# Splitting the weight transfers of one expert by rows in a hybrid attention and mixture-of-experts block

## Chip, cores and metric

The kernel runs on one core of a Trainium2 chip. The metric is the device time of one execution in microseconds (us), here the median of three runs. The profile is of one execution, with its own time.

## What is computed

One decoder block on 256 tokens of width 1024 in float32. Two attention branches (dilated, and a sliding window with sinks) share one input projection, are gated and added to `x`; then comes a mixture of 32 experts in 4 groups, of which each token uses two, and a last norm. The part that matters here:

```python
def hier_moe(h, w_group, b_group, w_router, b_router, w_e_gate, w_e_up, w_e_down):
    ...
    out = jnp.zeros_like(hf)
    for e in range(N_EXPERTS):
        a = jax.nn.silu(hf @ w_e_gate[e]) * (hf @ w_e_up[e])
        out = out + gates[:, e:e + 1].astype(hf.dtype) * (a @ w_e_down[e])
    return out.reshape(b, t, d)
```

`w_e_gate` and `w_e_up` are 1024 x 512 for each expert, `w_e_down` is 512 x 1024: 6 MB an expert, 192 MB in all.

## The kernel before

The first part of the program (projection, attention, output projection, routing) takes a little less than half of the span. The second part goes over the 32 experts (NE = 32) one after the other. For each, up to 32 of its tokens are gathered, multiplied by the gate and up weights (`gateup`, tile `gu`), activated, turned (`finish`, tile `atp`), multiplied by the down weights (tile `dn`), scaled, and added into the four accumulators `quad`. Every matmul is recorded at L132, a helper. For the last two experts some matmuls on no new data are put between the others (`busy`, tile `idle`). Behind the last expert stand the norm and four stores.

The weights lie in HBM so that each expert is three pieces of 2 MB, each of 128 rows (one for each partition) of 16 KB in one run: two pieces of `w_e_gu` (gate and up together, half of the depth each) and one of `w_e_down`. In SBUF a piece goes to a tile `ew` of 128 partitions x 4096 float32. The places for these tiles form a ring of large buffers, which fills up as the first part lets go of them. `prefetch(n)` takes the next n pieces of `chunk_items`, each into the next place of the ring, and calls `fill`, which issues the transfers on SyncE's queue (SP). One transfer carries a whole piece; only for the last expert (e = NE - 1 = 31) is a piece cut, by columns: each `w_e_gu` piece into two of 1 MB, the `w_e_down` piece into one of 1 MB and two of 512 KB. The loop over the experts calls `prefetch(2)` after the gate and up products of an expert and `prefetch(1)` after its down product. After expert 30, the gain of the last norm is fetched into a tile `gf` (L1107). The framework puts the waits in: a transfer waits for its place to be free and for a semaphore of its own, and the products wait for all transfers into the tile that they read. The semaphores that transfers raise are used in turn.

Transfers of another shape stand at the start of the program: among them 128 rows of 512 B into `cs` and 8 rows of 512 B into `grow`, both on ScalarE's queue (ACTq, q10 in the profile), and 8 rows into `frow` on SyncE's (q1).

Of the kernel before, what the change touches and what calls it, by code (L numbers as in the profile page):

```python
# [17 lines left out]
P = 128  # L18
# [5 lines left out]
NE = 32  # L24
# [60 lines left out]
def tile_hybrid_block(  # L85
# [12 lines left out]
    V, A, PE, SP = nc.vector, nc.scalar, nc.tensor, nc.sync  # L98
# [558 lines left out]
    chunks = {}  # L657
    nchunk = [0]

    def fill(t, e, what, i):  # L660
        if what == 0:
            parts = 2 if e == NE - 1 else 1
            for j in range(parts):
                n = 2 // parts
                SP.dma_start(
                    t[:, 2048 * n * j:2048 * n * (j + 1)],
                    w_e_gu[e, i, :, n * j:n * (j + 1)].rearrange("p k u r c -> p (k u r c)"))
        else:
            for c0, c1 in (((0, 2), (2, 3), (3, 4)) if e == NE - 1 else ((0, 4),)):
                SP.dma_start(t[:, 1024 * c0:1024 * c1], w_e_down[e, :, c0:c1, :].rearrange("p c o -> p (c o)"))  # L670

    def next_place(name):
        nchunk[0] += 1
# [13 lines left out]
    def prefetch(n):  # L687
        for _ in range(n):
            m = nchunk[0]
            if m >= len(chunk_items):  # L690
                return
            e, what, i = chunk_items[m]
            t = next_place(f"ew{m}")
            fill(t, e, what, i)
            for h in range(2):
                chunks[(e, what, 2 * i + h)] = t[:, 2048 * h:2048 * h + 2048]
# [471 lines left out]
```

## Time and profile before

| what | value |
|---|---|
| median of 3 runs | 747.11 us (745.70 to 747.63) |
| profiled execution, own time | 745.13 us |
| its span, first to last instruction | 743.3 us |
| TensorE matmul busy | 625.0 us, 84% |
| VectorE, ScalarE busy | 296.0 us, 224.3 us |
| moved by DMA | 249.86 MB, mean 336 GB/s |

The profile's times count from the first instruction. The DMA share of a stretch is the mean busy share of the core's 16 DMA engines; it can come out a little over 1. The time to landing of a transfer counts from its issue to the last of its completions. The profile doesn't say on which of the 16 engines a packet ran.

### The profile page before, as it was taken

How to read it: one execution, taken by the hardware profiler on the slowest of the kernel's cores; microseconds unless marked ns; L12 is line 12 of the kernel's file. 1: busy time of each engine (PE TensorE's matmuls, PEld its weight loads, DVE VectorE, ACT ScalarE, POOL GpSimd, SP SyncE). 2: the span in 40 equal slices, each digit the busy share in tenths (PEclk: the TensorE clock that was granted, in tenths of full speed). 3: DMA queues.
4: the chain of work that ended last, by engine and by line, in shares of the span. 5: the costliest groups of instructions: out<-in, count | busy, mean ns of one | idle time of the engine just before them, and what ended most of it. 6: DMA issues, size and time to landing. Idle time of an engine off the chain costs nothing.

```text
span 743.3 us, 14685 instructions
## 1 busy us (share of the span) xinstructions
PE 625.0 (84%) x6416; PEld 459.2 (62%) x6416; DVE 296.0 (40%) x753; ACT 224.3 (30%) x448; POOL 2.1 (0%) x10
## 2 busy tenths in 40 slices
PE   9999999999999999999988777677676867777772
PEld 8999988888998998655545334344333534433331
DVE  6554767985788566532223112111211111111103
ACT  6444566775788444210101001000000000000004
POOL 0000000000000000000000000000000000000000
PEclk9999999999999999999999789989879887978797
DMA  8746346336537978999999999999999999999993
GB/s 325 282 176 227 142 142 225 116 115 237 217 114 304 381 276 309 405 395 429 427 425 428 426 424 428 425 427 425 428 429 422 428 427 427 427 426 427 428 410 113
DMA packets 25940, 249.86 MB, mean 336 GB/s; under 512 B 5120, under 2 KB 6544, under 8 KB 8336
## 3 DMA queue, kind: packets, MB, share of 16 engines
q1 hardware_dynamic: 25712, 248.81, 82.4%
q8 instruction: 52, 0.85, 0.5%
q14 instruction: 16, 0.13, 0.0%
q10 hardware_dynamic: 160, 0.07, 0.0%
HBM read 247.82 MB, written 1.05 MB: 335 GB/s over the span
## 4 chain that ended last, share of the span: by engine, by line
DMA 50%; PE 24%; DVE 5%; ACT 5%; issue 1%; SPq 0%; DVEq 0%
DMA ew<-in_w_e_gu_dram 31%; DMA ew<-in_w_e_down_dram 19%; PE acc L132 12%; PE gu L132 4%; PE quad L132 2%; DVE set_split L258 2%; ACT set_probs L514 1%; PE dn L132 1%; PE ga L132 1%; DVE set_probs L525 1%; PE dpv L132 1%; PE dtp L594 1%; ACT set_split L257 1%; DVE set_qs L410 1%; DVE set_probs L512 1%
## 5 line engine op out<-in xcount | busy, mean ns | idle before, releaser
L132 PE MATMUL gu<-ew,xes 128*32 128x256 f32 x2048 | 151.0, 427 | 43.1 <-DMA ew<-in_w_e_gu_dram 42.9
L132 PE MATMUL acc<-set_hT,set_split 128*128 128x256 f32 x1200 | 151.3, 281 | 0.8 <-DVE set_qa L410 0.8
L132 PEld LDWEIGHTS acc<-set_hT,set_split 128*128 128x128 f32 x1200 | 142.1, 188 | 2.7 <-DVE set_qa L410 1.0
L132 PEld LDWEIGHTS gu<-ew,xes 128*32 128x32 f32 x2048 | 67.5, 120 | 104.8 <-DMA ew<-in_w_e_gu_dram 56.4
L258 DVE TENSOR_TENSOR set_split<-set_raw,set_split 128x1024 fp32r<-128x1024 f32 (+1 forms) x84 | 100.2, 1198 | 33.8 <-ACT set_split L257 31.3
L257 ACT CAST set_split<-set_raw 128x1024 fp32r<-128x1024 f32 (+1 forms) x84 | 86.3, 1029 | 42.0 <-PE acc L132 41.1
L946 DVE TENSOR_TENSOR set_raw<-set_raw,gu 128x128 f32<-128x128 f32 x32 | 9.2, 286 | 193.0 <-ACT set_raw L943 192.9
L132 PE MATMUL dn<-ew,set_raw 128*32 128x256 f32 x1024 | 75.1, 435 | 9.8 <-DMA ew<-in_w_e_down_dram 9.4
L943 ACT ACTIVATE set_raw<-gu 128x128 f32<-128x128 f32 x32 | 8.9, 277 | 218.4 <-PE gu L132 218.4
L132 PEld LDWEIGHTS dn<-ew,set_raw 128*32 128x32 f32 x1024 | 34.9, 122 | 35.3 <-issue 10.8
L972 ACT ACTIVATE y_hi<-dn,gsl 128x256 fp32r<-128x256 f32 x32 | 15.2, 473 | 97.2 <-PE dn L132 97.2
L132 PE MATMUL ga<-set_raw 128*128 128x128 f32 x256 | 37.0, 304 | 5.2 <-DVE set_raw L959 4.2
L132 PEld LDWEIGHTS ga<-set_raw 128*128 128x128 f32 x256 | 33.7, 212 | 9.0 <-DVE set_raw L959 6.9
L974 DVE SCALAR_TENSOR_TENSOR y_lo<-dn,gsl,y_hi 128x256 fp32r<-128x256 f32 x32 | 15.4, 481 | 59.6 <-ACT y_hi L972 59.6
L881 ACT ACTIVATE xes<-ga,fcol 128x128 f32<-128x128 f32 x32 | 11.6, 367 | 76.0 <-DVE xes L883 76.0
L132 PE MATMUL acc<-set_split,set_hT 128*128 128x512 f32 x144 | 34.1, 393 | 0.4 <-DVE set_ks L420 0.2
L913 DVE TENSOR_SCALAR set_raw<-cs,pos 128x128 f32<-128x128 f32 x64 | 17.8, 281 | 37.9 <-PE ct L132 37.9
L132 PE MATMUL quad<-y_hi,cts 32*128 32x256 f32 x256 | 23.3, 350 | 9.1 <-ACT y_hi L972 9.1
L132 PEld LDWEIGHTS acc<-set_split,set_hT 128*128 128x128 f32 x144 | 26.7, 188 | 6.7 <-DVE set_split L258 0.6
L132 PEld LDWEIGHTS quad<-y_hi,cts 32*128 32x128 f32 x256 | 13.6, 200 | 22.1 <-ACT y_hi L972 20.6
L132 PE MATMUL quad<-y_lo,cts 32*128 32x256 f32 x256 | 21.5, 344 | 6.9 <-DVE y_lo L974 3.4
L138 PE MATMUL atp<-cs,set_raw 128*128 128x128 f32 x32 | 11.1, 346 | 19.0 <-DVE set_raw L946 18.2
(201 smaller groups left out, 632.8 us busy)
## 6 DMA issues: line engine op xcount, KB each, us to landing
ew<-in_w_e_gu_dram SPq DMA_DIRECT2D x62, 2048.0 KB, 39.1
ew<-in_w_e_down_dram SPq DMA_DIRECT2D x31, 2048.0 KB, 39.3
set_raw<-in_w_in_dram SPq DMA_DIRECT2D x29, 1024.0 KB, 5.3
set_raw<-in_w_br_swa_dram SPq DMA_DIRECT2D x4, 1024.0 KB, 4.9
set_raw<-in_w_out_dram SPq DMA_DIRECT2D x4, 1024.0 KB, 6.1
ew<-in_w_e_gu_dram SPq DMA_DIRECT2D x4, 1024.0 KB, 33.1
set_raw<-in_w_br_dil_dram SPq DMA_DIRECT2D x2, 1024.0 KB, 5.1
set_x<-in_x_dram SPq DMA_DIRECT2D x2, 512.0 KB, 4.4
```

The lines of the kernel that those rows point to most:

```text
L132: i = PE.matmul(o, lhsT, rhs, start=start, stop=stop, skip_group_check=True)
L138: i = PE.transpose(o, src, ident)
L257: order(A.copy(w[:, 0, :, :ncol], r))
L258: order(V.tensor_tensor(out=w[:, 1, :, :ncol], in0=r, in1=w[:, 0, :, :ncol].bitcast(F32), op=ALU.subtract))
L410: V.scalar_tensor_tensor(out=lo, in0=sv, scalar=cs[own, j:j + 1], in1=hi.bitcast(F32), op0=ALU.mult, op1=ALU.subtract)
L512: V.tensor_tensor_reduce(out=v, in0=s, in1=dist, scale=float(scale), scalar=init, op0=ALU.add, op1=ALU.min, accum_out=nm[:, i:i + 1])
L881: A.activation(dst, src, AF.Copy, scale=col)
L913: eq = V.tensor_scalar(dd[:, t, :].rearrange("p (g s) -> p g s", g=REP), cs[:, C_CNT:C_CNT + CAP].unsqueeze(1).to_broadcast([P, REP, CAP]) ...
L943: A.activation(ac, gu[:, 0:P], AF.Silu)
L946: V.tensor_tensor(out=ac, in0=ac, in1=gu[:, P:2 * P], op=ALU.mult)
L972: A.activation(y_hi, dn[:, 0:256], AF.Copy, scale=gsl)
L974: V.scalar_tensor_tensor(out=y_lo, in0=dn[:, 0:256], scalar=gsl, in1=y_hi.bitcast(F32), op0=ALU.mult, op1=ALU.subtract)
```

## The change

For the last expert but one (e = NE - 2 = 30), each of its three pieces goes out as three transfers in place of one: rows 0 to 111, rows 112 to 119, and rows 120 to 127. The bytes and the tiles are the same. All other transfers stay as they are.

```diff
+    def whole(t, src):
+        SP.dma_start(t, src)
+
+    def by_rows(t, src):
+
+        for a, b in ((0, 112), (112, 120), (120, P)):
+            SP.dma_start(t[a:b], src[a:b])
+
     def fill(t, e, what, i):
+        put = by_rows if e == NE - 2 else whole
         if what == 0:
             parts = 2 if e == NE - 1 else 1
             for j in range(parts):
                 n = 2 // parts
-                SP.dma_start(
+                put(
                     t[:, 2048 * n * j:2048 * n * (j + 1)],
                     w_e_gu[e, i, :, n * j:n * (j + 1)].rearrange("p k u r c -> p (k u r c)"))
         else:
             for c0, c1 in (((0, 2), (2, 3), (3, 4)) if e == NE - 1 else ((0, 4),)):
-                SP.dma_start(t[:, 1024 * c0:1024 * c1], w_e_down[e, :, c0:c1, :].rearrange("p c o -> p (c o)"))
+                put(t[:, 1024 * c0:1024 * c1], w_e_down[e, :, c0:c1, :].rearrange("p c o -> p (c o)"))
```

## Rows read from the trace of the kernel before

**Rows 1.** The page's 40 slices: busy tenths of TensorE, DMA share, GB/s

```profile
PE   9999999999999999999988777677676867777772
...
DMA  8746346336537978999999999999999999999993
GB/s 325 282 176 227 142 142 225 116 115 237 217 114 304 381 276 309 405 395 429 427 425 428 426 424 428 425 427 425 428 429 422 428 427 427 427 426 427 428 410 113
```

**Rows 2.** Chain of waits, 560 to 730 us: start us, length us, what

```profile
585.41 39.31 DMA ew<-in_w_e_down_dram
...
624.78 40.07 DMA ew<-in_w_e_gu_dram
...
664.90 3.47 PE gu L132 x32
...
670.19 39.12 DMA ew<-in_w_e_gu_dram
709.30 0.02 issue
709.32 19.84 DMA ew<-in_w_e_down_dram
729.16 0.04 issue
729.20 0.68 PE dn L132 x8
```

**Rows 3.** Waits of SyncE's queue, 560 to 716 us: total us, times, longest

```profile
SPq L665 <- DMA ew<-in_w_e_gu_dram: 50.7, 11, 5.6
SPq L670 <- DMA ew<-in_w_e_gu_dram: 45.1, 10, 4.5
SPq L665 <- DMA ew<-in_w_e_down_dram: 41.0, 9, 4.9
SPq L1107 <- DMA ew<-in_w_e_down_dram: 4.6, 1, 4.6
SPq L670 <- DMA ew<-in_w_e_down_dram: 4.6, 1, 4.6
SPq L665 <- PE ct L132: 0.5, 2, 0.3
SPq L670 <- PE ct L132: 0.3, 1, 0.3
SPq L670 <- PE dn L132: 0.2, 1, 0.2
```

**Rows 4.** Timeline of SyncE's queue, issues between 664 and 715 us

```profile
664.92 0.33 SPq L665 DMA_DIRECT2D ew<-in_w_e_gu_dram  x1
...
675.09 0.33 SPq L670 DMA_DIRECT2D ew<-in_w_e_down_dram  x1
679.99 0.33 SPq L665 DMA_DIRECT2D ew<-in_w_e_gu_dram  x1
...
704.43 0.33 SPq L670 DMA_DIRECT2D ew<-in_w_e_down_dram  x1
709.32 0.33 SPq L670 DMA_DIRECT2D ew<-in_w_e_down_dram  x1
714.27 0.33 SPq L1107 DMA_DIRECT2D gf<-in_g_final_dram  x1
```

**Rows 5.** Stretches: busy us of each engine, TensorE clock, DMA share, GB/s

```profile
620.00:719.00 99.00, 73.36 (x861) 40.57 (x853) 14.24 (x49) 6.72 (x18) 0.00 (x0) 0.83 1.01 426
...
723.00:724.00 1.00, 0.33 (x3) 0.12 (x2) 0.00 (x0) 0.00 (x0) 0.00 (x0) 1.00 0.94 385
724.00:725.00 1.00, 0.81 (x16) 0.42 (x16) 0.00 (x0) 0.00 (x0) 0.00 (x0) 1.00 0.83 340
725.00:726.00 1.00, 0.72 (x11) 0.32 (x4) 0.29 (x1) 0.65 (x2) 0.00 (x0) 1.00 0.59 229
726.00:727.00 1.00, 0.80 (x8) 0.56 (x12) 0.29 (x1) 0.99 (x2) 0.00 (x0) 1.00 0.50 188
727.00:728.00 1.00, 0.88 (x20) 0.34 (x16) 0.00 (x0) 0.12 (x1) 0.00 (x0) 1.00 0.51 205
728.00:728.40 0.40, 0.40 (x8) 0.10 (x8) 0.00 (x0) 0.00 (x0) 0.00 (x0) 1.00 0.49 195
728.40:728.80 0.40, 0.18 (x4) 0.00 (x0) 0.00 (x0) 0.00 (x0) 0.00 (x0) 1.00 0.49 195
728.80:729.20 0.40, 0.00 (x0) 0.00 (x1) 0.00 (x0) 0.00 (x0) 0.00 (x0) 1.00 0.35 143
729.20:730.00 0.80, 0.64 (x8) 0.16 (x8) 0.00 (x0) 0.09 (x1) 0.00 (x0) 1.00 0.23 92
```

**Rows 6.** DMA queues, 340 to 729 us: packets, MB, share of 16 engines

```profile
q8 instruction: 28, 0.46, 0.5%
```

**Rows 7.** DMA view, 0 to 20 us: a queue, and ScalarE's two issues

```profile
q10 hardware_dynamic: 160, 0.07, 1.8%
...
cs<-c_small_dram ACTq DMA_DIRECT2D x1, 64.0 KB, 3.5
...
grow<-in_g_mix_dram ACTq DMA_DIRECT2D x1, 4.0 KB
```

**Rows 8.** The page's DMA issues: count, KB each, median us to landing

```profile
ew<-in_w_e_gu_dram SPq DMA_DIRECT2D x62, 2048.0 KB, 39.1
ew<-in_w_e_down_dram SPq DMA_DIRECT2D x31, 2048.0 KB, 39.3
set_raw<-in_w_in_dram SPq DMA_DIRECT2D x29, 1024.0 KB, 5.3
```

## Prediction

> **What bounds the kernel now.** I read the page's slices first [rows 1]. From a third of the span on, the DMA row stands at 9 in every slice and the GB/s row between about 405 and 429, while TensorE's own row falls to 7 and 6: the second half is a stream of weights, and the engines wait for it. The chain of waits agrees [rows 2]: from 585 us it is transfers of some 39 us laid end to end, with a few microseconds of TensorE between two of them, and the last one, the final part of the last expert's down weights, lands at 729.16 us. What comes behind it (the last down product, the output product, the norm, the store) takes the rest of the 743.3 us, 14.1 us, and the change touches none of it. So the question is only when that last part lands.
>
> Next the queue that issues the transfers. SyncE waits almost always for a landing, and for TensorE only 1.0 us in all over 156 us [rows 3]. The issue times say which landing: the three pieces of the last expert but one are issued at 664.92, 670.19 and 675.09, the transfers eight issues behind them at 704.43, 709.32 and 714.27 [rows 2, 4], and the second of these follows the landing at 709.31 by 0.02 us [rows 2]. A transfer lands some 39 us after its issue [rows 8] and a piece takes 4.9 us, which is eight pieces. Eight transfers are in flight, whatever their size, and each landing lets one more go.
>
> Last the tail, cut fine [rows 5]. Up to 719 us the DMA share is 1.01 at 426 GB/s. From 723 it falls, and from 726 to 728.8 it stays at 0.49 to 0.51 with 188 to 205 GB/s. Half of the engines have nothing left, and the other half doesn't speed up: 205 over 0.51 is 402 GB/s for all sixteen, under the 426 of before (the rows are smaller there). So an engine has its own pace, 426/16/1.01 = 26.4 GB/s, and a row of 16 KB takes it 0.62 us. How far is the late half behind? Missing share from 723 to 728.4: 0.06 + 0.17 + 0.41 + 0.50 + 0.49 + 0.4 x 0.51 = 1.83 us of all engines, 3.7 us of half of them, so the early half ends at 724.7 on average. The late half's share after 728.4 is 0.4 x 0.49 + 0.4 x 0.35 + 0.8 x 0.23 = 0.52, 1.0 us of half of them, so it ends at 729.4. The lag is 4.7 us. A cause that fits: in the 389 us before, 28 instruction packets took 0.5% of sixteen engines' time [rows 6], which is 31 us, 3.9 us for each of eight engines and 1.9 for each of sixteen. The last transfer lands with the late half.
>
> **The change, part by part.** Expert 30 has three pieces, 128 rows of 16 KB each. Now a piece is one transfer, 8 rows for each of sixteen engines. After it is 112 rows, then 8, then 8.
>
> *112 rows.* Sixteen divides 112: 7 rows an engine, 0.62 us less on each engine and piece, 1.85 us over three.
>
> *The 8-row transfers.* The trace has an 8-row transfer: early on, ScalarE's queue moved 128 rows of 512 B and 8 more, in 160 packets [rows 7]. 136 of these are rows; the other 24 are completions, 16 for the large transfer and 8 for the small one. So 8 rows go to eight engines, one each. [...] Taking the same eight both times, a piece gives eight engines 9 rows and eight engines 7, and three pieces move 3 rows, 1.85 us, from one half to the other.
>
> *Which half.* No row names engines. If the loaded half is the early one, the late half ends 1.85 us sooner and the early half 1.85 us later, with 4.7 - 3.7 = 1.0 us of lag left: the last landing moves by -1.85. If it is the late one, by +1.85. I take the early one. The order in which the trace keeps packets that start together leans to it, but no view prints that, so it is a judgment: 5 to 1.
>
> *Six more issues on SyncE.* 0.33 us each [rows 4], 2 us in all, against 146 us of waits for landings in the 156 us [rows 3]: nothing.
>
> *Three landings to wait for.* TensorE's first product on a piece of expert 30 now waits for three transfers; the next products and expert 30's tail are queued behind it. From 620 to 719 us TensorE is busy 73 of 99 us [rows 5], so a shift of 2 us there is absorbed as long as the last expert's transfers aren't late themselves: nothing.
>
> *The eight places in flight.* The nine transfers fill more than the eight places, so what follows is issued later. The third part of expert 30's down piece must wait for the landing of the 112 rows of its first piece (704.43 before, some 0.6 sooner now), and the last expert's first transfer goes right behind it, at about 704.2 instead of 679.99 [rows 4]. When are they needed? Expert 30's down piece landed just ahead of 714.27; the late half gets there at about 712.4, the early half at 714.3 - 4.7 + 1.85 = 711.4. So the lead shrinks from 34 us to 7. A transfer of 1 MB into an idle queue needs 5.3 us to land [rows 8], of which 2.5 are its own data at 426 GB/s, so some 2.9 us of lead are enough. Nothing is lost; without that cover it would be 2 to 5 us once.
>
> *An 8-row transfer's own pace.* Its rows go to eight neighbouring partitions, from eight engines at a time. No large transfer of that shape stands in the trace. From below: 0.62 us, the pace that an engine holds whether eight or sixteen of them run [rows 5]. From above: the eight rows get no further than two at a time, four turns of 0.62, 2.46 us. I take the lower end, because rows 5 are nearest to it: there eight engines run and each keeps its pace.
>
> The sum against the profiled execution: last landing 729.16 - 1.85 = 727.3, span 741.5, its own time 745.13 - 1.85 = 743.3. That execution lies 1.98 us under the median of 747.11; from the median, the forecast is **745.3 us**, 0.25% faster. What a measurement here can tell from no change is about 0.3%, 2.2 us, so this would mostly read as no change.
>
> **Rivals.**
>
> *The 8-row transfers block (slower).* At the upper end each of the six costs 1.85 us more on the loaded half, 11.1 us. That half starts 4.7 us early and takes 1.85 us of added rows: -4.7 + 1.85 + 11.1 = +8.2 us, about 755. If the two small transfers of a piece overlap fully, 16 rows in four turns, the extra is 1.23 us a piece, 3.7 in all, and the end moves by +0.9; if the 112 rows, whose shares no longer fall as those of 128 do, hurt each other as well by half a row per engine and piece, another 1 us on top of the 8.2. It decides from an extra of 4.7 - 1.85 = 2.85 us, 0.48 us a small transfer. For it: the constant pace of rows 5 was seen only where each engine has a share of a transfer of 128 rows. Against it: nothing in the trace slows down when engines run out of step. [...]
>
> *The other half is loaded.* +1.85 us, 749.0. For it: no row names engines. Against it: only the judgment above.
>
> *Rows follow partitions.* If the engine goes by the partition that is written and not by the count, the sixteen rows of the two small transfers fall to the engines that had them before, and every engine still has 8 rows: 747.1. Against it: the eight completions in rows 7, which fit one row an engine.
>
> *The queue runs dry.* If the lead of 7 us is not enough, 2 to 5 us once: about 750. Against it: the 5.3 us of rows 8.
>
> **How the numbers follow.** Forecast (early half loaded, own pace) 0.42; blocking 0.40, spread over 748 to 757; other half 0.07; rows by partition 0.06; dry queue 0.05. The likeliest, 745.3, has its own range of 744.3 to 746.3, from the scatter of the three runs. About 3 in 10 of it would read faster than 0.3%: 0.13. No change: the rest of it 0.29, rows by partition 0.06, most of the other half 0.05, and a little of the blocking case where its transfers overlap, 0.02: 0.42. Slower: 0.45. The range runs from 744.3 to 757: it leaves out the lower edge of the forecast and the blocking case's far end, in all under 2 in 10.
>
> **What will show it.** Forecast right: the half-share stretch of rows 5 shrinks from about 4.7 us to about 1, the last down part lands near 727.3, and the stretch from 699 to 714 keeps 426 GB/s. Blocking: in that stretch the DMA share stays near 1 while the GB/s fall well under 426, the half-share stretch stays or grows, and the last part lands after 732. Other half: the same pace, and a half-share stretch of 8 us. By partition: the tail as before. Dry: a hole in the DMA share near 711. In every case the last expert's first transfers are issued from about 704, in a burst; if they still go at 680, the count of eight in flight is wrong. What makes the forecast wrong first is the price of an 8-row transfer.

## The result, and the profile after

The changed kernel takes 771.1 us (median of 6 runs) against 747.5 us before: 1.032 times as long, 95% interval 1.030 to 1.034, so 24 us slower. The forecast was 745.3 us, in a range from 744.3 to 757. The profiled execution took 769.46 us, with a span of 767.6.

The page's GB/s row of the changed kernel, 40 slices of 19.2 us, to be laid beside the one in [rows 1]:

```profile
GB/s 315 279 184 201 165 164 167 110 149 291 150 119 421 300 311 365 364 429 423 427 426 426 427 425 426 426 427 425 429 427 423 429 426 427 427 427 237 210 328 86
```

From the 19th slice to the 36th both rows read 422 to 429; before that the slices are hard to compare one by one, since they are 19.2 us long here and 18.6 before. Then two slices stand at half, and a third at 328. The chain of waits of the changed kernel over its end (start us, length us, what), which answers to [rows 2]; the first line is expert 29's down piece, which is whole:

```profile
661.69 47.60 DMA ew<-in_w_e_down_dram
...
709.30 28.08 DMA ew<-in_w_e_down_dram
...
737.40 15.70 DMA ew<-in_w_e_down_dram
753.10 0.04 issue
753.14 0.68 PE dn L132 x8
```

The last down part lands at 753.10 instead of 729.16, 23.9 us later, and what follows takes 14.5 us instead of 14.1. So nearly all of the loss lies ahead of the last landing. The stretches of the changed kernel (busy us of each engine, granted TensorE clock, DMA share, GB/s), which answer to [rows 5]:

```profile
680.00:690.00 10.00, 6.89 (x83) 3.65 (x87) 1.97 (x7) 0.75 (x2) 0.00 (x0) 0.83 1.01 426
690.00:700.00 10.00, 3.79 (x60) 1.83 (x56) 0.00 (x0) 0.00 (x0) 0.00 (x0) 0.88 1.04 290
700.00:710.00 10.00, 4.48 (x35) 2.44 (x31) 1.07 (x4) 0.28 (x1) 0.00 (x0) 0.50 1.00 202
710.00:720.00 10.00, 7.87 (x75) 4.11 (x70) 0.48 (x1) 0.47 (x1) 0.00 (x0) 0.50 1.02 224
720.00:730.00 10.00, 4.97 (x42) 2.23 (x34) 0.00 (x0) 0.00 (x0) 0.00 (x0) 0.67 0.99 194
730.00:740.00 10.00, 4.35 (x39) 2.13 (x35) 1.07 (x4) 0.28 (x1) 0.00 (x0) 0.67 0.99 296
740.00:745.00 5.00, 5.00 (x70) 2.79 (x63) 0.48 (x1) 0.47 (x1) 0.00 (x0) 0.81 1.00 415
```

The last two columns are the ones to read together. The share stays at 0.99 to 1.04, so all sixteen engines have a packet in hand nearly all the time; but in the five stretches from 690 to 740 us they move 194 to 296 GB/s instead of 426. The queue has not run dry: the packets take about twice as long. The traces hold each packet's time and show it directly: of the 259 rows of 16 KB that start between 700 and 720 us none takes less than 0.65 us, and the median is 1.18; in the kernel before, all but 2 of the 522 that start between 680 and 700 take 0.61 to 0.65 us. What is missing against 426 in the five stretches is 136 + 224 + 202 + 232 + 130 = 924 GB/s over 10 us each, which at 426 GB/s are 21.7 us. Another 1.7 us were there before: expert 30's first transfer goes at 666.59 in this execution and at 664.92 before. Together that is 23.4 of the 23.9.

The issues of expert 30's nine transfers and of the next, in the timeline of SyncE's queue of the changed kernel:

```profile
666.59 0.33 SPq L666 DMA_DIRECT2D ew<-in_w_e_gu_dram  x1
671.45 0.28 SPq L666 DMA_DIRECT2D ew<-in_w_e_gu_dram  x1
...
698.47 0.32 SPq L666 DMA_DIRECT2D ew<-in_w_e_down_dram  x1
709.30 0.27 SPq L666 DMA_DIRECT2D ew<-in_w_e_down_dram  x1
717.64 0.27 SPq L666 DMA_DIRECT2D ew<-in_w_e_down_dram  x1
718.01 0.83 SPq L661 DMA_DIRECT2D ew<-in_w_e_gu_dram  x2
```

The ninth transfer goes at 717.64 and the last expert's first right behind it at 718.01 (679.99 before [rows 4]): eight in flight, as read, only that the landing it waits for came some 14 us later than I had worked out.

### The profile page after: what moved, and what is told of

It is laid out like the page before. It is cut to its first block, busy times and chain, and to the rows that moved or that the text cites. A ratio compares the mean times of both kernels' runs of the same rounds, so it can differ in the third digit from the quotient of the medians.

```text
span 767.6 us, 14694 instructions
## 1 busy us (share of the span) xinstructions
PE 624.8 (81%) x6416; PEld 458.6 (60%) x6416; DVE 296.0 (39%) x753; ACT 224.4 (29%) x448; POOL 2.1 (0%) x10
## 4 chain that ended last, share of the span: by engine, by line
DMA 48%; PE 25%; DVE 6%; ACT 5%; issue 1%; SPq 0%; ACTq 0%; DVEq 0%
DMA ew<-in_w_e_gu_dram 26%; DMA ew<-in_w_e_down_dram 22%; PE acc L132 11%; PE gu L132 5%; PE dn L132 2%; PE quad L132 2%; DVE set_split L258 2%; ACT set_probs L514 1%; PE ga L132 1%; DVE set_probs L525 1%; ACT set_split L257 1%; DVE set_qs L410 1%; PE dtp L594 1%; DVE set_probs L512 1%; ACT L514 1%
## 5 line engine op out<-in xcount | busy, mean ns | idle before, releaser
L132 PE MATMUL gu<-ew,xes 128*32 128x256 f32 x2048 | 154.0, 434 | 60.9 <-DMA ew<-in_w_e_gu_dram 60.8
L132 PE MATMUL dn<-ew,set_raw 128*32 128x256 f32 x1024 | 72.8, 425 | 15.1 <-DMA ew<-in_w_e_down_dram 15.0
L138 PE MATMUL atp<-cs,set_raw 128*128 128x128 f32 x32 | 11.1, 346 | 19.0 <-DVE set_raw L955 18.2
L138 PEld LDWEIGHTS atp<-cs,set_raw 128*128 128x128 f32 x32 | 4.6, 144 | 36.7 <-DVE set_raw L955 33.7
## 6 DMA issues: line engine op xcount, KB each, us to landing
ew<-in_w_e_gu_dram SPq DMA_DIRECT2D x4, 1024.0 KB, 18.6
```

Source lines behind the costliest of these rows:

```text
L132: i = PE.matmul(o, lhsT, rhs, start=start, stop=stop, skip_group_check=True)
L138: i = PE.transpose(o, src, ident)
```

## The experiments

Each is timed against runs of the kernel before. "Loss" is the ratio less 1, times the median of before in those runs; the 95% interval of the ratio stands in brackets. The theories that the results are held against are named in the expectations: A to C ahead of e1, D and E ahead of e3, A1 and A2 ahead of g1, M1 ahead of g3. A "group" is four neighbouring partitions, counted from 0.

### Which part of the cut costs, and is it the shape

**e1**: 112 and 16 rows, no 8-row transfers.

```diff
-        for a, b in ((0, 112), (112, 120), (120, P)):
+        for a, b in ((0, 112), (112, P)):
```

> Expert 30's three pieces as 112 rows and 16 rows each: every engine has 7 + 1 rows, as many as with 128. Theory A (neighbouring partitions share a way in, and rows written by several engines at a time to one group of four neighbours hold one another up, in the 112 rows as well as in the small transfers): most of the 24 us stays, +12 to +22 us against the kernel before, and the GB/s stand near half of 426 over some 30 us. Theory B (only the two 8-row transfers block, by eight engines on two groups): they are gone and the load is even, 0 to +5 us (the 16 rows still go to four groups). Theory C (more transfers than the eight places in flight: the queue runs dry): six transfers fit, 0 to +1 us, and no fall of the GB/s.

1.026 (1.023 to 1.029), a loss of 19.3 us. Its stretches:

```profile
680.00:690.00 10.00, 5.04 (x75) 2.80 (x79) 1.48 (x6) 0.28 (x1) 0.00 (x0) 1.00 1.01 428
...
710.00:720.00 10.00, 6.11 (x51) 3.30 (x51) 0.48 (x1) 0.47 (x1) 0.00 (x0) 0.50 1.00 220
720.00:730.00 10.00, 4.58 (x35) 2.29 (x35) 0.00 (x0) 0.00 (x0) 0.00 (x0) 0.50 0.98 220
```

Most of the loss is there without a single 8-row transfer, with 7 + 1 rows for each engine, if both transfers are dealt evenly, and six transfers in eight places. Theories B and C fall as the main cause; the imbalance of 9 and 7 rows, which the prediction was about, has little to do with the time. The run has three 16-row transfers as well; what they cost by themselves it doesn't show.

**e2**: only the down piece is cut.

```diff
-        put = by_rows if e == NE - 2 else whole
+        put = by_rows if e == NE - 2 and what == 1 else whole
```

> Only expert 30's down piece as 112, 8 and 8 rows, the other two whole. Theories A and B (each piece pays by itself): about a third of the loss of three pieces, +6 to +9 us; less by up to 4.7 us if the lag between the halves hides a part. Theory C (the nine transfers against eight places): three transfers leave five places for whole pieces, 0 to +1 us.

1.014 (1.011 to 1.017), 10.3 us, somewhat more than the third that was expected. One cut piece is enough for a loss.

**e3** and **e4**: only the down piece, as eight transfers of 16 rows, to 16 neighbours or to every eighth partition.

```diff
+        for r in range(8):
+            SP.dma_start(t[16 * r:16 * r + 16], src[16 * r:16 * r + 16])   # e3
+            SP.dma_start(t[r:P:8], src[16 * r:16 * r + 16])                # e4
```

> Only expert 30's down piece, as eight transfers of 16 neighbouring partitions: one row for each of sixteen engines, four groups of four. Theory A: four rows take turns in each group, 2.46 us a transfer in place of 0.62, so up to 19.7 us for the piece in place of 4.9: +7 to +15 us. Theory B as far as it speaks of eight engines on two groups says the same, four rows a group. Theory D (any transfer that isn't of 128 rows is slow, or many small ones are, whatever partitions they reach): the same loss as in the run with every eighth partition, whatever it is. Theory E (the order in which HBM is read): also the same as there, since the source rows are the same.

> The same eight transfers of 16 rows with the same source rows, but each goes to every eighth partition (the weights land in other partitions than the reference wants, which changes the result of expert 30). [...] Theories D and E: the same as the run with neighbours.

1.0125 (1.010 to 1.015) and 1.012 (1.009 to 1.016), 9.4 and 9.1 us: no difference that these runs show, which is what theories D and E had said, and not what A says of rows that lie eight partitions apart. But the pair is inconclusive, for a reason that a stretch of each shows, e3's first:

```profile
710.00:720.00 10.00, 3.93 (x30) 1.93 (x30) 0.00 (x0) 0.00 (x0) 0.00 (x0) 0.67 0.68 156
```

```profile
710.00:720.00 10.00, 6.65 (x58) 2.87 (x50) 0.22 (x1) 0.28 (x1) 0.00 (x0) 0.73 0.76 199
```

The DMA share is 0.68 and 0.76. Eight transfers of 256 KB fill the eight places with 2 MB, and here the engines did run out of packets. That mixes with whatever the partitions cost, in both.

### Where rows are written, or how they are read

**f1** and **f2**: all pieces whole; eight extra 8-row transfers, one behind each of the eight pieces ahead of the last expert's, to a place that nobody reads (it takes one place of the ring, in both runs and in g1, g2 and h3 below). The two differ in the partitions alone.

```diff
+            if 0 <= r < 8:      # behind the r-th of the eight pieces; sp8[0] is a place of the ring
+                SP.dma_start(sp8[0][8 * r:8 * r + 8, :], w_e_gu[0, 0, 8 * r:8 * r + 8]...)                          # f1
+                SP.dma_start(sp8[0][32 * (r // 4) + r % 4:32 * (r // 4) + 32:4, :], w_e_gu[0, 0, 8 * r:8 * r + 8]...)  # f2
```

> All pieces whole, as in the kernel before. Behind each of the eight pieces ahead of the last expert's goes one more transfer of 8 rows of 16 KB, eight neighbouring partitions each time, into a place of the ring that nobody reads (64 rows, 1 MB, that the computation doesn't need). Eight engines get one row more each time, 4.9 us over all. Theory A (rows that several engines write to one group of four neighbours at a time hold one another up): each small transfer costs its engines up to 2.46 us and jostles the whole pieces beside it, +8 to +18 us. Theory E (the order in which HBM is read) and theory D (small transfers cost by their number): the same as the run with every fourth partition.

> The same eight extra transfers with the same source rows on the same eight engines and in the same places of the queue; only the partitions differ: each time every fourth one of 32, so each row of a transfer is alone in its group of four neighbours. Theory A: no jostling; if the eight engines are the early half, their 4.9 us of added rows fill the lag of 4.7 and the time moves by 0 to +1 us; if they are the late half, +4.9 us. Theories D and E: as much as the run with neighbours.

f1: 1.019 (1.016 to 1.023), 14.5 us. f2: 1.006 (1.004 to 1.008), 4.6 us. The same bytes from the same rows, eight rows each time. The stretches of f1, then of f2:

```profile
680.00:700.00 20.00, 12.81 (x135) 6.25 (x127) 1.97 (x7) 0.75 (x2) 0.00 (x0) 0.74 1.01 342
700.00:720.00 20.00, 10.73 (x125) 5.73 (x125) 1.55 (x5) 0.75 (x2) 0.00 (x0) 0.83 1.01 366
```

```profile
680.00:700.00 20.00, 13.94 (x151) 6.74 (x151) 2.04 (x7) 1.03 (x3) 0.00 (x0) 0.74 1.01 430
700.00:720.00 20.00, 14.20 (x155) 7.96 (x159) 2.62 (x9) 0.75 (x2) 0.00 (x0) 0.83 1.00 419
726.00:728.00 2.00, 1.83 (x22) 0.88 (x20) 0.00 (x0) 0.00 (x0) 0.00 (x0) 1.00 0.87 354
728.00:730.00 2.00, 1.29 (x18) 0.71 (x18) 0.00 (x0) 0.16 (x1) 0.00 (x0) 1.00 0.75 297
730.00:732.00 2.00, 1.48 (x21) 0.86 (x20) 0.58 (x2) 1.61 (x3) 0.00 (x0) 1.00 0.22 82
732.00:734.00 2.00, 1.01 (x16) 0.16 (x8) 0.00 (x0) 0.00 (x0) 0.00 (x0) 1.00 0.13 53
```

Eight neighbours slow the whole stream, to 342 and 366 GB/s at a share of 1.01; every fourth partition leaves it at 430 and 419. So the 8-row transfer's price is a matter of its partitions, and D and E fall there. The trace of f1 tells how far the slowing reaches: between 680 and 700 us rows of 16 KB that take over 0.65 us fill 231 us of engine time, more than the 160 that eight engines have in 20 us. So more than eight engines are slowed, and with that some that carry no extra row, if the small transfers always take the same eight. In f2 such rows fill 2.3 us.

Which half the small transfers load has to be read from f2's tail, for its loss of 4.6 us alone would fit the 4.9 that were expected of the late half better than the 0 to 1 of the early one. Before, the share stood at 0.50 and 0.51 from 726 to 728 [rows 5]. With 4.9 us more on the late half it would have stood there until about 734. Here it is 0.87 from 726 to 728 and 0.75 from 728 to 730, so the early half took the rows. What the 4.6 us are made of is the end of it: a share of 0.13 over 732 to 734 is two engines, which end some 4 us behind the others. Why these two, no run shows.

**f3** and **f4**: expert 30 reads one HBM row for all partitions, cut as in the changed kernel (f3) or whole (f4).

```diff
+        for a, b in ((0, 112), (112, 120), (120, P)):                                # f3
+            SP.dma_start(t[a:b], src[0:1].to_broadcast([b - a, src.shape[1]]))       # f3
+        SP.dma_start(t, src[0:1].to_broadcast([P, src.shape[1]]))                    # f4
```

> The changed kernel (112, 8 and 8 rows for all three pieces of expert 30), but every transfer of expert 30 reads one and the same HBM row for all its partitions (expert 30's weights are wrong by that). Theory A (it is where the rows are written): the loss stays, +20 to +26 us. Theory E (it is the order or the pitch in which the engines read HBM): the loss goes or changes by more than half.

> The control to the run with one source row: whole pieces as in the kernel before, expert 30's read from one HBM row. Both theories: 0 to +1 us, if reading one row again and again costs nothing by itself; what it costs is to be taken off the run with 112, 8 and 8 rows.

1.034 (1.030 to 1.038), 25.3 us, and 1.0005 (0.998 to 1.003), 0.4 us. The loss stays when every row is read from one place (25.3 us against the 23.6 of the changed kernel), and reading so costs nothing by itself. So E falls for the 112 rows too: it is the writing side.

### Who holds up whom

**g1**, **g2** and **h3**: f2 with other partitions for the same eight extra transfers.

```diff
-                SP.dma_start(sp8[0][32 * (r // 4) + r % 4:32 * (r // 4) + 32:4, :], ...)                 # f2
+                SP.dma_start(sp8[0][4 + 32 * (r // 4) + r % 4:36 + 32 * (r // 4):4, :], ...)             # g1
+                SP.dma_start(sp8[0][r:64:8, :], ...)                                                     # g2
+                SP.dma_start(sp8[0][64 + 32 * (r // 4) + r % 4:64 + 32 * (r // 4) + 32:4, :], ...)       # h3
```

> The run with eight extra 8-row transfers on every fourth partition, moved on by four partitions: each row of a transfer is still alone in its group of four, but the group is the one that the next engine writes in the whole pieces (if consecutive rows go to consecutive engines). Theory A1 (an engine that writes to a group which another engine is writing at that time slows both, whole pieces included): each extra row meets a whole row, +5 to +14 us, nearer to the run with neighbours than to the unmoved one. Theory A2 (only rows of one and the same transfer hold one another up): the same as the unmoved one, +4 to +5 us.

> [...] By A2 with every group of four on its own: +4 to +5 us, as the run with every fourth partition.

> [...] Theory A2 (only rows of one transfer hold one another up): as with partitions 0 to 63, +4 to +5 us and 426 GB/s.

g1: 1.019 (1.016 to 1.022), 14.4 us. g2: 1.0185 (1.016 to 1.021), 13.8 us. h3: 1.019 (1.0145 to 1.023), 14.0 us, well over the +4 to +5 of A2. g1's rows are as far apart as f2's; they are moved by four partitions, one group. That alone takes the time from +4.6 to +14.4. So it is not enough that the rows of one transfer keep apart: A2 falls. A1 fits, by which a row that goes to a group which another engine is filling slows both; it stays an explanation, since no row names the engine that fills a group. h3, with its rows in partitions 64 to 127, is as slow. A stretch of g1, then two of h3:

```profile
680.00:700.00 20.00, 12.73 (x119) 6.08 (x119) 1.97 (x7) 0.75 (x2) 0.00 (x0) 0.62 1.00 356
```

```profile
680.00:700.00 20.00, 13.68 (x119) 6.83 (x119) 2.03 (x7) 0.75 (x2) 0.00 (x0) 0.53 1.00 320
700.00:720.00 20.00, 15.23 (x132) 7.66 (x125) 1.55 (x5) 0.75 (x2) 0.00 (x0) 0.53 1.00 332
```

Between 680 and 700 us the rows over 0.65 us fill 234 us of engine time in g1 and 266 in h3, again more than eight engines have. But f1, whose extra rows stay in partitions 0 to 63, has nearly as much, 231: which engines a meeting slows, no run shows. g2 fits as well: all but one of the rows of each of its transfers go to another group than in f2.

A simpler rival would be that only the number of groups counts that a transfer reaches. It would fit the four runs of the next section. Here it falls: f2, g1, g2 and h3 reach eight each, and lose 4.6, 14.4, 13.8 and 14.0 us.

### How rows are dealt to engines

**g3**, **g4**, **h1** and **h2**: expert 30's three pieces as two transfers of 64 rows or four of 32, to neighbours or spread.

```diff
+        for a, b in ((0, 64), (64, P)): SP.dma_start(t[a:b], src[a:b])                                    # g3
+        for r in range(2): SP.dma_start(t[r:P:2], src[64 * r:64 * r + 64])                                # g4
+        for r in range(4): SP.dma_start(t[r:P:4], src[32 * r:32 * r + 32])                                # h1
+        for r in range(4): SP.dma_start(t[32 * r:32 * r + 32], src[32 * r:32 * r + 32])                   # h2
```

> Expert 30's three pieces as rows 0 to 63 and 64 to 127: four rows for each of sixteen engines in each transfer, the load even. Theory M1 (consecutive rows go to consecutive engines, so sixteen engines write sixteen neighbouring partitions, four a group): as slow as 112 and 16 rows, +17 to +23 us. [...] Theory D (what is not 128 rows is slow, however it lies): as 112 and 16 rows.

> The same two transfers of 64 rows from the same source rows, but to the even and to the odd partitions (expert 30's rows land elsewhere than the reference wants). Theory M1: sixteen engines write over 32 partitions at a time, two a group of four counted with nothing else: +9 to +15 us, well under the run with 64 neighbours. [...] Theory D: the same as that run.

> Expert 30's three pieces as four transfers each, of 32 source rows in a run to every fourth partition (the rows land elsewhere than the reference wants). [...] Theory M1 (consecutive rows to the sixteen engines in turn): two engines a way in, +5 to +11 us. [...]

> The control to the run with every fourth partition: the same number, size and source of transfers, 32 neighbouring partitions each. [...] If the number or the size of the transfers did the harm, or the rows per engine, it would be the same as with every fourth partition.

g3: 1.024 (1.022 to 1.027), 18.2 us. g4: 0.9997 (0.998 to 1.002), no loss. h2: 1.026 (1.022 to 1.0305), 19.7 us. h1: 1.0001 (0.9985 to 1.002), no loss, with twelve transfers against eight places. One stretch of each; h2, then h1:

```profile
710.00:720.00 10.00, 5.67 (x62) 2.83 (x55) 0.48 (x1) 0.47 (x1) 0.00 (x0) 0.67 1.00 216
```

```profile
710.00:720.00 10.00, 8.89 (x125) 4.75 (x115) 1.22 (x5) 0.75 (x2) 0.00 (x0) 0.95 1.00 415
```

The same number of transfers, of the same size, from the same rows, all engines busy in both: 216 or 415 GB/s by the partitions alone. In h2 every row of 16 KB that starts between 700 and 720 us takes over 0.65 us (median 1.22), in h1 24 of 291. (h1 has a stretch at 377 GB/s and a share of 0.95 from 700 to 710 us; its time shows no loss.) So neither a cut into four nor twelve transfers cost anything that the time shows, and theory D falls for good. M1 hits g3 (+17 to +23 expected, 18.2 measured) and misses g4 and h1, where it had put two engines at a group, +9 to +15 and +5 to +11 us. What the four runs show is that parts which each go to every second or every fourth of the 128 partitions keep the pace (415 GB/s in g4 and in h1 from 710 to 720 us), and that parts of 64 or 32 neighbours do not (228 in g3, 216 in h2). By which rule rows are dealt to engines they don't show, since no row names the engines. How 112 rows are dealt, no run shows either; that they lose in the same way as 32 neighbours is read from the likeness of the two (220 GB/s in e1 and 216 in h2 from 710 to 720 us, at a share of 1.00).

No version came out faster than the kernel before: g4 and h1 equal it.

## Why the prediction was wrong, by its steps

**The bound, and the way to the last landing: right.** Of the 24.3 us between the two spans 0.4 lie behind the last landing and 1.7 ahead of expert 30's first transfer; the rest lies in the stream of weights. One reading was loose: the stream fills the slices from the 17th on, four tenths of the span and not a third, and the last slice is outside it.

**The eight places in flight: right in kind.** The ninth transfer and the last expert's first went out back to back. The lead was enough, since the DMA share stayed at 0.99 to 1.04 from 690 to 740 us; e3 and e4 show what it looks like when it is not. What I worked out as 704.2 was 718.01, because the landings were late. (That the 5.3 us of [rows 8] are those of an idle queue, no row shows; nothing came to depend on it.)

**The step that failed: an engine's own pace for every row, wherever it is written.** The sum gave each row of the cut transfers 0.62 us, in the 112 rows as in the 8. From 700 to 720 us of the changed kernel the rows of 16 KB took 1.18 us (median), and expert 29's whole piece beside them was held up as well: 47.6 us to its landing instead of 39.3.

**The 112 rows: the larger part, and mis-sized in the forecast and in the rival.** In the sum they were a saving of 1.85 us; in the rival I let them cost "half a row per engine and piece", 1 us. e1, which has them and no 8-row transfers, loses 19.3 us. Its three 16-row transfers are in that; e3 has eight of them and loses 9.4 us, so three are worth some 3.5 us by that, or 5.3 if the lag of 4.7 us hid a part of e3's. By this estimate 14 to 16 us stay with the 112 rows. Why they are so slow is argued from h2, which runs at a like rate: rows that are dealt otherwise than in a transfer of 128 would make engines write where others write. No row names the engines, so this stays an argument.

**An 8-row transfer's own pace: wrong too.** I took the lower end, 0.62 us, "because rows 5 are nearest to it: there eight engines run and each keeps its pace". Those engines write the partitions that a whole piece gives them, and rows 5 cannot show what happens elsewhere. f1 and f2 do: 14.5 against 4.6 us for eight such transfers with the same bytes. The upper end, two rows at a time and 2.46 us a transfer, no run shows either: the 9.9 us between f1 and f2 are 1.2 for each of the eight, what the whole pieces beside them lose included. In the changed kernel the step from e1 to the full cut is only 23.6 - 19.3 = 4.3 us, though, so they look like the smaller part.

**The blocking rival, 0.40: right in its signs, not in its sum.** The share stayed near 1, the GB/s fell and the last part landed after 732, as it had said. But it put nearly all of its price on the 8-row transfers. So it came to +8.2, its range ended at 757, and the measured loss is three times that.

**Which half: right.** The small transfers load the early half, by f2's tail: a share of 0.87 and 0.75 from 726 to 730 us, where 0.50 and 0.51 stood from 726 to 728 before. That both small transfers of a piece take the same eight engines, on which the sum's 9 and 7 rows rest, no run shows; f2's tail fits it.

**The gain of 1.85 us.** No run shows it. h3 speaks against it: with eight rows at a time in partitions 64 to 127 the stream fell to 320 GB/s. Those rows were added there, not moved, and no run shows which half writes there, so that a moved row gains nothing is argued from it and not shown.

**Rows follow partitions, the other half, a dry queue.** If the engine went by the partition, each row would have kept its engine, and g3, h2 and the changed kernel itself should have cost nothing. The other half's 1.85 us and the dry queue's 2 to 5 are both far below what was measured, and the share of 1 excludes the second.

## What to carry to other kernels

These runs are best explained so, though no row names an engine: a stream of whole 128-partition transfers keeps its pace (426 GB/s) because each engine writes partitions that no other engine writes at that time. Before cutting a transfer by rows, ask where the rows of each part land, not only how many each engine gets. A cut that spreads each part over all partitions (64 rows to every second or 32 to every fourth) was free here; one into neighbours (64 or 32) halved the rate of the whole stream while its pieces moved (211 to 228 GB/s in g3 and 215 to 216 in h2, from 700 to 730 us). And when the DMA share stays at 1 while the GB/s fall, as here at 0.99 to 1.04 and 194 to 296, look first for such meetings and not for a missing issue.

## What the runs showed that I had not expected

- Holding up spreads to a transfer that isn't cut: in the changed kernel expert 29's down piece, whole and issued ahead of every cut one, takes 47.60 us to land, where such pieces took 39.3 before [rows 8].
- Four partitions are enough: f2 and g1 differ by a shift of four, 4.6 against 14.4 us.
- Twice or four times as many transfers, of 64 or 32 rows, cost nothing when each goes to every second or every fourth partition (0.9997 and 1.0001).
- TensorE's granted clock stood at 0.50 from 700 to 720 us of the changed kernel. In the 10 us before it had been busy 3.8, and in these two stretches 4.5 and 7.9 of 10 us. From 745 to 754 us it read 1.00 again.
